# A Trainium2 encoder layer: three heads' attention in single buffers beside the projections instead of two, one head beside the Fourier branch instead of two

## The chip, the cores and the metric

The kernel runs on one core of a Trainium2 chip. The metric is the device time of one execution in microseconds (us). The kernel before takes 2184.91 us, the median of 3 runs (2184.82 to 2186.43). In the text PE is TensorE, DVE VectorE, ACT ScalarE, POOL GpSimd; SP is the engine that issues nearly all DMA transfers. Each engine works through its own instructions in order.

## What is computed

One layer of an encoder with 1024 tokens and width 1024, all in float32: a feed-forward block, a mixer, a second feed-forward block and a norm. The mixer has two branches, a Fourier transform over tokens and channels, and differential attention with four heads: each head has two components of width 64 with a softmax each, the second is subtracted from the first with a factor, and the difference weighs values of width 128.

```python
def diff_attention(q, k, v, positions, rel_bias, lam):
    ...
        s1 = jnp.einsum('bhqd,bhkd->bhqk', qblk[0], k[0]) * scale + bias
        s2 = jnp.einsum('bhqd,bhkd->bhqk', qblk[1], k[1]) * scale + bias
        attn = jax.nn.softmax(s1, axis=-1) - lam * jax.nn.softmax(s2, axis=-1)
        return jnp.einsum('bhqk,bhkv->bhqv', attn, vh)

def hybrid_mixer(h, ...):
    proj = h @ w_in
    u_f, q, k, v, g_a, g_b = jnp.split(proj, cuts, axis=-1)
    y_a = fourier_branch(u_f) @ w_fourier_out
    o = diff_attention(q, k, v, positions, rel_bias, lam)
    o = rms_norm(o, subln_g, SUBLN_EPS) * (1.0 - lambda_init)
    y_b = o.reshape(B, S, V_WIDTH) @ w_attn_out
    merged = jax.nn.sigmoid(g_a) * y_a + jax.nn.sigmoid(g_b) * y_b
    return merged @ w_out
```

## The kernel before

**Products.** Operands are split into a high part of 12 bits and the rest (`split`: a copy on ACT, L134, and a subtraction, L135, mostly on DVE), and a product takes three matmuls. The large products go by a form of Strassen's with seven block products (`seven_products`; its matmuls are L378, twelve to a product and half of the tokens, and DVE adds the results up in L386). `project(tiles, fn, cols, hook)` computes two tiles of 128 columns of `h @ w_in` for all tokens; after each of its seven products it calls `hook` once, which takes a step of a generator. So the generators' instructions are written between those of the products.

**What sets the order.** The written order is where a scheduler starts: it places each instruction on its engine by a timeline of its own, with waits where memory is reused. The order that results is fixed when the kernel is built. Memory has names: `xtile(j)` is x_j, `ntile(j)` n_j, `htile(j)` h_j; two things with one name can't live at once. `rh` hands out small tiles in turn.

**One tile of queries** (128 of the 1024, number g = 8 h + i of head h) takes these steps. `scores(g, c)`: matmuls of the component's queries and keys (L1148), on DVE the sum with the bias and its maximum (L1151), on ACT the exponentials (L1154). `combine(g)`: the factor (L1159, L1160), then s1 + factor s2, by ACT (L1165) and POOL (L1166), or for odd tiles of the later heads by DVE alone (L1163). `turn(g)`: eight transposes on PE (L1182) and a split. Then the weights by values: `weigh0`, one tile, 16 matmuls of 256 columns (L1224), summed (L1227, L1228) and stored to `o_d` in DRAM; or `weigh`, two tiles, 24 matmuls (L1195), and `back`, two transposes (L1206).

**Heads 0 and 1** run in `first_heads`, stepped by the hooks of the projections (8, 9), (2, 6), (3, 7), eight pairs of gates and (10, 11). Their exponentials stand in x5 and x6 for even tiles, x5 and x7 for odd ones, so that x5 has one tile at a time. **Head 2's** operands are made by `head_prep(2)` beside (12, 13), and its first tiles by `prime` beside (14, 15). `head_prep(h)` loads each half of queries and keys twice from DRAM (`twice`, L1075), copies it on ACT (L1083, L1092), subtracts on POOL (L1084, L1093), and transposes the values (L1113). It writes x0 to x4, for head 3 n4, n5 and x5.

**Heads 2 and 3** have four buffers (n0, n1, n2, n6) in turn and work beside the generator `fourier`, whose 40 steps `fill` spreads over their 16 tiles. The steps of `hgen` between them are `head_prep(3)` in head 2 and `early_norms` (the norms of heads 0 to 2) in head 3. Then come y_b, the gates and the merge (first matmul L562), the output projection and the second feed-forward block.

## Time and profile before

| | |
|---|---|
| median of 3 runs | 2184.91 us |
| the profiled execution, its span | 2188.2 us |
| PE busy | 2020.4 us, 92% |
| DVE busy | 1632.8 us, 75% |
| POOL busy | 1113.3 us, 51% |
| ACT busy | 951.0 us, 43% |

A profile records one execution with every instruction's start and end on each engine. Busy shares are means over the whole span, in which stages with different limits follow each other; the views by window and the timelines of the engines tell what holds in one stage. The seven products' L378 alone takes 1151.9 us of PE in 5256 matmuls. The granted clock is the mean of PE's clock, 1.00 being full.

### The profile page before, as it was taken

How to read it: one execution, taken by the hardware profiler on the slowest of the kernel's cores; microseconds unless marked ns; L12 is line 12 of the kernel's file. 1: busy time of each engine (PE TensorE's matmuls, PEld its weight loads, DVE VectorE, ACT ScalarE, POOL GpSimd, SP SyncE). 2: the span in 40 equal slices, each digit the busy share in tenths (PEclk: the TensorE clock that was granted, in tenths of full speed). 3: DMA queues.
4: the chain of work that ended last, by engine and by line, in shares of the span. 5: the costliest groups of instructions: out<-in, count | busy, mean ns of one | idle time of the engine just before them, and what ended most of it. 6: DMA issues, size and time to landing. Idle time of an engine off the chain costs nothing. (4 is left out here: it accounts for less than half of the span.)

```text
span 2188.2 us, 27538 instructions
## 1 busy us (share of the span) xinstructions
PE 2020.4 (92%) x9433; PEld 1642.4 (75%) x9433; DVE 1632.8 (75%) x2266; ACT 951.0 (43%) x1687; POOL 1113.3 (51%) x788
## 2 busy tenths in 40 slices
PE   5999999997988899999999799888999999979987
PEld 4987788875866777777776577667888888857775
DVE  8866566579897966666758987978766656598995
ACT  6423333233434544767646652345332333333345
POOL 5622233347579663343364652787432323275586
PEclk9999999999999899999999989999999999999998
DMA  4222511160421244353366547312222221151302
GB/s 139 89 85 85 149 52 55 57 221 0 132 71 53 87 150 130 98 168 94 111 190 205 160 133 273 107 66 82 75 82 82 72 58 58 56 185 49 121 15 87
DMA packets 155190, 228.90 MB, mean 105 GB/s; under 512 B 15968, under 2 KB 65280, under 8 KB 155048
## 3 DMA queue, kind: packets, MB, share of 16 engines
q1 hardware_dynamic: 148920, 215.85, 30.9%
q10 hardware_dynamic: 4608, 8.39, 1.0%
q0 software_dynamic: 1520, 2.88, 0.5%
q8 instruction: 75, 1.23, 0.2%
q14 instruction: 67, 0.55, 0.1%
HBM read 181.95 MB, written 49.31 MB: 106 GB/s over the span
## 5 line engine op out<-in xcount | busy, mean ns | idle before, releaser
L378 PE MATMUL p<-n,op 128*128 128x512 f32 (+1 forms) x5256 | 1151.9, 379 | 23.3 <-DVE r L386 11.3
L378 PEld LDWEIGHTS p<-n,op 128*128 128x128 f32 x5256 | 945.9, 191 | 214.6 <-issue 13.0
L134 ACT ACTIVATE op<-r 128x512 fp32r<-128x512 f32 x472 | 291.7, 628 | 556.6 <-PE p L378 255.6
L135 DVE TENSOR_TENSOR op<-r,op 128x512 fp32r<-128x512 f32 x453 | 398.7, 892 | 134.8 <-ACT op L134 129.7
L386 DVE TENSOR_TENSOR r<-p,r 128x512 f32<-128x512 f32 (+1 forms) x462 | 288.9, 639 | 270.9 <-PE p L378 265.8
L218 POOL TENSOR_TENSOR r<-r,r 128x512 f32<-128x512 f32 x189 | 276.8, 1474 | 246.9 <-DVE op L135 196.5
L562 PE MATMUL b<-n,op 128*128 128x512 f32 x1080 | 265.6, 402 | 41.3 <-DVE n L135 21.9
L562 PE MATMUL p<-n,op 128*128 128x512 f32 x1068 | 261.6, 403 | 28.5 <-DVE n L135 23.1
L562 PEld LDWEIGHTS b<-n,op 128*128 128x128 f32 x1080 | 204.4, 192 | 98.1 <-DVE n L135 33.0
L562 PEld LDWEIGHTS p<-n,op 128*128 128x128 f32 x1068 | 206.0, 195 | 79.0 <-DVE n L135 27.2
L222 POOL TENSOR_TENSOR r<-r,r 128x512 f32<-128x512 f32 x63 | 84.9, 1348 | 325.4 <-DVE x L774 80.2
L135 DVE TENSOR_TENSOR n<-n,n 128x512 fp32r<-128x512 f32 x142 | 174.7, 1239 | 4.7 <-ACT n L134 4.7
L503 POOL TENSOR_TENSOR n<-n,n 128x512 f32<-128x512 f32 x50 | 82.1, 1658 | 69.1 <-DVE n L135 28.7
L134 ACT ACTIVATE n<-n 128x512 fp32r<-128x512 f32 x156 | 95.3, 616 | 10.1 <-DVE n L1735 6.3
L1166 POOL TENSOR_TENSOR x<-x,x 128x1024 f32<-128x1024 f32 x16 | 38.8, 2426 | 109.8 <-ACT x L1165 101.7
L765 ACT ACTIVATE r<-r 128x512 f32<-128x512 f32 (+1 forms) x96 | 57.0, 596 | 84.8 <-DVE r L386 83.1
L134 ACT ACTIVATE op<-n 128x512 fp32r<-128x512 f32 x64 | 40.2, 629 | 99.5 <-PE b L562 41.7
L134 ACT ACTIVATE op<-x 128x512 fp32r<-128x512 f32 x68 | 42.8, 629 | 86.9 <-PE b L562 44.2
L591 POOL TENSOR_TENSOR n<-n,n 128x512 f32<-128x512 f32 x32 | 53.8, 1704 | 49.0 <-DVE n L597 49.0
L1148 PE MATMUL A<-x,x 128*128 128x512 f32 (+1 forms) x192 | 66.4, 432 | 6.5 <-ACT x L1092 4.1
L400 ACT ACTIVATE r<-p 128x512 f32<-128x512 f32 (+1 forms) x66 | 36.6, 555 | 71.7 <-PE p L378 68.7
L135 DVE TENSOR_TENSOR op<-x,op 128x512 fp32r<-128x512 f32 x58 | 57.8, 997 | 6.6 <-ACT op L134 6.5
(291 smaller groups left out, 2486.5 us busy)
## 6 DMA issues: line engine op xcount, KB each, us to landing
r<-in_ffn_wg SPq DMA_DIRECT2D x96, 256.0 KB
r<-in_ffn_wu SPq DMA_DIRECT2D x94, 256.0 KB
n<-in_ffn_wd SPq DMA_DIRECT2D x88, 256.0 KB
proj_d<-r SPq DMA_DIRECT2D x56, 256.0 KB
h_d<-r SPq DMA_DIRECT2D x32, 256.0 KB
rh<-proj_d SPq DMA_DIRECT2D x64, 128.0 KB
x<-bias_d SPq DMA_DIRECT2D x16, 512.0 KB
r<-in_w_gate SPq DMA_DIRECT2D x32, 256.0 KB
```

The lines of the kernel that those rows point to most:

```text
L134: act.activation(hi, src, AF.Copy)
L135: eng.tensor_tensor(out=lo, in0=src, in1=hi, op=ALU.subtract)
L218: pool.tensor_tensor(out=b[o], in0=b[x], in1=b[y], op=ALU.subtract)
L222: pool.tensor_tensor(out=b["s1"], in0=b[2], in1=b[3], op=ALU.add)
L378: pe.matmul(ps, lhsT=w[wi][:, d * P:(d + 1) * P], rhs=xn[b][xi][:, d, cols], start=(m == 0), stop=(m == 11))
L386: dve.tensor_tensor(out=o, in0=x, in1=y, op=ALU.add)
L503: eng.tensor_tensor(out=y, in0=v, in1=w, op=op)
L562: pe.matmul(ps[p], lhsT=wa[ai][:, p * P:(p + 1) * P], rhs=wb[bi], start=(j == 0 and m == 0), stop=(j == nj - 1 and m == 2))
L591: pool.tensor_tensor(out=new[1], in0=old[1], in1=v, op=ALU.add)
L765: act.activation(c, c, AF.Silu)
L1148: pe.matmul(ps[:, ns], lhsT=qq, rhs=kk[:, ns], start=(n == 0), stop=(n == 1))
L1166: pool.tensor_tensor(out=s1, in0=s2, in1=s1, op=ALU.add)
```

## The change

Three heads instead of two run in `first_heads`, in x5, x6, x7, with their sums stored to `o_d`; only head 3 has the four buffers and runs beside the Fourier branch, so `fill` spreads its 40 steps over 8 tiles. `head_prep(3)` stands at the end of `first_heads` and uses x0 to x4 like the other heads. A new hook `beside` takes 129 steps (as many as `first_heads` has) over the 91 hooks of 13 projections. The values (10, 11) are projected earlier, (12, 13) is among the 13; `prime` is now for head 3. `early_norms` runs from the start of the loop and loads three heads from `o_d`, into n7, n4, n5. The norms' results for heads 0 and 1 are in memory of their own (e0, e1, e2, and x5), no longer in x0 to x3. The weight stream is ordered like the products; a scratch memory for descriptors is set to 4096 bytes. All comments and docstrings are gone, which shifts line numbers by two or three. The diff without them:

```diff
+HEAD_STEPS = 129
+NB_HEADS = H - 1
...
-    o_d = dram.tile([2, TT, P, P], F32, name="o_d")
+    o_d = dram.tile([NB_HEADS, TT, P, P], F32, name="o_d")
...
-    for hp in (0, 4, 2, 3):
+    for hp in (0, 4, 2, 5, 3):
         qkv(hp, EARLY[2][3] if hp == 0 else "")
     for dm in range(DT):
         seven(lambda b, dm=dm: fetch(a["w_gate"][dm, b]))
-    qkv(5)
...
     def head_prep(h):
-        if h == 3:
-            two = [ntile(4 + j, [P, 2, S]) for j in range(2)]
-            stk[h] = [two[j // 2][:, j % 2, :] for j in range(4)] + [xtile(5, [P, S], F32R)]
-        else:
-            stk[h] = [xtile(j, [P, S], F32R) for j in range(5)]
+        stk[h] = [xtile(j, [P, S], F32R) for j in range(5)]
...
-    G0 = 2 * TT
+    G0 = NB_HEADS * TT
...
     def head_norm(h, halves=(0, 1)):
         if oT[h] is None:
-            oT[h] = [htile(q, [P, S]) if h == 2 else xtile(2 * h + q, [P, S], F32R) for q in range(2)]
+            oT[h] = [htile(q, [P, S]) if h == 2 else xtile(2 * h + q, [P, S], F32R) if h == 3 else
+                     T(big, f"e{2 * h + q}", [P, S], F32R) if h + q < 2 else xtile(5, [P, S], F32R) for q in range(2)]
...
     def early_norms():
-        o_first()
+        for k in range(H - 1):
+            o_s[k] = (o23[:, 0], *n45)[k]
+            sp.dma_start(out=o_s[k], in_=o_d[k].rearrange("t p c -> p t c"))
+        yield
         head_scale(0, (H - 1) * TT)
...
     def first_heads():
-        for _ in range(3):
+        for _ in range(6):
             yield
-        for h in range(2):
+        for h in range(NB_HEADS):
             yield from head_prep(h)
...
             weigh0(g0 + TT - 1)
             yield
+        yield from head_prep(NB_HEADS)
+
+    hgen = first_heads()
+    pace = [0, 0]
+
+    def beside():
+        pace[0] += 1
+        while pace[1] < pace[0] * HEAD_STEPS // (13 * NBLK):
+            pace[1] += 1
+            step(hgen)
...
-    hgen = first_heads()
-    project((8, 9), None, hook=each(hgen))
-    for h in range(2, H):
-        project((h, 4 + h), None, hook=each(hgen))
+    project((8, 9), None, hook=beside)
+    project((2, 6), None, hook=beside)
+    project((10, 11), None, hook=beside)
+    project((3, 7), None, hook=beside)
     for dm in range(DT):
-        project((16 + dm, 24 + dm), AF.Sigmoid, hook=each(hgen))
-    project((10, 11), None, hook=each(hgen))
-    for _ in hgen:
-        pass
-    hgen = head_prep(2)
-    project((12, 13), None, hook=each(hgen))
+        project((16 + dm, 24 + dm), AF.Sigmoid, hook=beside)
+    project((12, 13), None, hook=beside)
     for _ in hgen:
         pass
...
     project((14, 15), None, hook=each(prime()))
     o23 = ntile(7, [P, 2, TT, P], F32)
-    o_s[2], o_s[3] = o23[:, 0], o23[:, 1]
-
-    def o_first():
-        o01 = ntile(11, [P, 2, TT, P], F32)
-        for h in range(2):
-            sp.dma_start(out=o01[:, h], in_=o_d[h].rearrange("t p c -> p t c"))
-            o_s[h] = o01[:, h]
+    o_s[3] = o23[:, 1]
+    n45 = [ntile(j, [P, TT, P], F32) for j in (4, 5)]
...
     fgen = fourier()
-    hgen = head_prep(3)
+    hgen = early_norms()
...
     for g in range(G0 + 2, NG + 2):
         h, i = divmod(g, TT)
-        if i == 0 and g < NG:
-            if hgen is not None:
-                for _ in hgen:
-                    pass
-            hgen = head_prep(h + 1) if h + 1 < H else early_norms()
...
-        if g < NG and (i > 0 if h + 1 < H else i > 1):
+        if g < NG and i > 1:
             step(hgen)
...
-    nc = bacc.Bacc("TRN2", target_bir_lowering=False, num_devices=1)
+    nc = bacc.Bacc("TRN2", target_bir_lowering=False, num_devices=1, dynamic_dma_scratch_size=4096)
```

What that does to the order on the engines is shown at three places. A row is an instruction: its line, its operation, out<-in and the shape; the numbers behind a tile's name tell its uses apart.

The first is DVE around the last sum of the projections, the row of L386 that reads p_11050; the rows of L1151 are sums of scores, A being the scores. Before:

```order
L386 TENSOR_TENSOR r_1485_10927<-p_11050,r_1485_10927 128x512
L1151 ISA n_1512_11079,nms<-A_11167,n_1512_11079 128x1024
L1151 ISA nms 128x1
L1151 ISA n_1480_10904,nms<-A_11290,n_1480_10904 128x1024
L1151 ISA nms 128x1
L135 TENSOR_TENSOR n_1509_11064<-b_11065,n_1508_11063 128x4x128
L135 TENSOR_TENSOR n_1509_11064<-b_11072,n_1508_11063 128x4x128
L1151 ISA n_1480_10904,nms<-A_11297,n_1480_10904 128x1024
L1151 ISA nms 128x1
L1159 RECIPROCAL ccs<-l2s 128x1
L1151 ISA n_1481_10906,nms<-A_11368,n_1481_10906 128x1024
L1151 ISA nms 128x1
```

The same place after, where lines are moved (L388 is the sum of the projections, L1148 that of scores, L1156, L1157 the factor, L1225 and L1211 the end of `weigh0`):

```order
L1148 ISA x_1000_8102,nms<-A_10491,x_1001_8103 128x1024
L1148 ISA nms 128x1
L137 TENSOR_TENSOR h_1402_10476<-b_10477,h_1401_10475 128x512
L137 TENSOR_TENSOR h_1402_10476<-b_10484,h_1401_10475 128x512
L1148 ISA x_1001_8103,nms<-A_10547,x_1001_8103 128x1024
L1148 ISA nms 128x1
L388 TENSOR_TENSOR r_1576_11456<-p_11579,r_1576_11456 128x512
L1156 RECIPROCAL ccs<-l2s 128x1
L1157 SCALAR_TENSOR_TENSOR ccs<-l1s,ccs,nlam 128x1
L1225 TENSOR_TENSOR rh_10515<-b_10498,rh_10515 128x128
L1211 ISA junk_10518,oss<-rh_10515 128x128
L1211 ISA oss 128x1
```

Before, sums of scores of three buffers (n_1512, n_1480, n_1481) follow each other there, between them the split of a transposed tile. After, one tile's two sums are in x_1000 and x_1001 (x5 and x6), and the end of `weigh0` of a tile of head 2 follows.

The second is POOL where head 3's operands are made: L1084 and L1093 subtract for queries and keys, L1166 combines a tile, L1283 to L1301 are the Fourier branch's folds. Before:

```order
L1166 TENSOR_TENSOR n_1480_10904<-n_1480_10904 128x1024
L1283 MEMSET r_1566_11337 128x512
L1283 MEMSET r_1567_11338 128x512
L1084 TENSOR_TENSOR n_1523_11123<-rh_11231,n_1523_11123 64x512
L1084 TENSOR_TENSOR n_1523_11123<-rh_11236,n_1523_11123 64x512
L1093 TENSOR_TENSOR x_1525_11125<-rh_11309,n_1524_11124 64x512
L1295 COPY r_1573_11395<-r_1566_11337 128x1
L1093 TENSOR_TENSOR x_1525_11125<-rh_11314,n_1524_11124 64x512
L1296 TENSOR_TENSOR r_1573_11395<-r_1566_11337,r_1567_11338 128x511
L1300 TENSOR_TENSOR r_1574_11398<-r_1573_11395,r_1567_11338 128x1 x2
L1301 TENSOR_TENSOR r_1574_11398<-r_1573_11395 128x255 x2
L1166 TENSOR_TENSOR n_1489_10947<-n_1489_10947 128x1024
```

After, with the same subtractions in L1085 and L1094, combines in L1163:

```order
L1163 TENSOR_TENSOR x_1000_8102<-x_1001_8103,x_1000_8102 128x1024
L1163 TENSOR_TENSOR x_1000_8102<-x_1002_8104,x_1000_8102 128x1024
L1085 TENSOR_TENSOR x_1537_11281<-rh_11286,x_1537_11281 64x512
L1085 TENSOR_TENSOR x_1538_11282<-rh_11291,x_1538_11282 64x512
L1085 TENSOR_TENSOR x_1537_11281<-rh_11322,x_1537_11281 64x512
L1085 TENSOR_TENSOR x_1538_11282<-rh_11327,x_1538_11282 64x512
L1094 TENSOR_TENSOR x_1541_11285<-rh_11332,x_1539_11283 64x512
L1094 TENSOR_TENSOR x_1541_11285<-rh_11337,x_1540_11284 64x512
L1094 TENSOR_TENSOR x_1541_11285<-rh_11362,x_1539_11283 64x512
L1094 TENSOR_TENSOR x_1541_11285<-rh_11367,x_1540_11284 64x512
L1163 TENSOR_TENSOR n_1571_11433<-n_1571_11433 128x1024
L1163 TENSOR_TENSOR n_1580_11476<-n_1580_11476 128x1024
```

Before, the subtractions stand one or two at a time among the folds and the combines of head 2. After, all eight stand in a row, behind the combines of head 2's last two tiles, which are in x5 (x_1000), and ahead of the first combine of head 3.

The third is SP at the same preparation, after; L1076 is `twice`, its two loads in one row, L1227 stores a tile of `weigh0`, L1107 loads values:

```order
L1227 DMA o_d<-rh_11023 128x128
L1227 DMA o_d<-rh_11120 128x128
L149 DMA r_1725_12273<-proj_d 128x512
L149 DMA r_1726_12275<-proj_d 128x512
L1076 DMA rh_11286<-proj_d 64x512 x2
L1227 DMA o_d<-rh_11257 128x128
L1076 DMA rh_11291<-proj_d 64x512 x2
L1076 DMA rh_11322<-proj_d 64x512 x2
L1531 DMA n_1606_11614<-o_d 128x8x128
L1076 DMA rh_11327<-proj_d 64x512 x2
L1076 DMA rh_11332<-proj_d 64x512 x2
L1076 DMA rh_11337<-proj_d 64x512 x2
```

The first pair of loads stands ahead of the store of head 2's last tile (rh_11257), the other seven behind it. Before, the pairs for head 3 stand among the loads of the bias, with no such store near them.

## Rows read from the trace of the kernel before

**Rows 1.** The page: span; TensorE's busy time, share, instructions, and its weight loads.

```profile
span 2188.2 us, 27538 instructions
...
PE 2020.4 (92%) x9433; PEld 1642.4 (75%) x9433; DVE 1632.8 (75%) x2266; ACT 951.0 (43%) x1687; POOL 1113.3 (51%) x788
```

**Rows 2.** Busy us (instructions) by engine and window, granted clock, DMA share, GB/s.

```profile
794.55:1169.40 374.85, 369.01 (x1728) 289.38 (x1729) 251.66 (x399) 218.77 (x340) 162.14 (x123) 1.00 0.46 143
1169.40:1259.70 90.30, 72.81 (x378) 53.24 (x377) 82.08 (x146) 57.80 (x113) 56.09 (x62) 0.90 0.53 164
1259.70:1384.60 124.90, 115.15 (x563) 92.47 (x564) 100.62 (x179) 46.55 (x84) 58.66 (x44) 0.92 0.56 193
1169.40:1384.60 215.20, 187.95 (x940) 145.72 (x939) 182.70 (x324) 104.36 (x197) 114.75 (x106) 0.91 0.55 181
```

**Rows 3.** PE's timeline: start us, us, what; both ends of the second stretch.

```profile
1166.35 3.03 PE L378 MATMUL p<-n,op 128*128 128x512 f32 x12
1169.22 1.04 PE L1182 MATMUL b<-ident,n 128*128 128x128 f32 x8
...
1384.62 7.64 PE L562 MATMUL p<-n,op 128*128 128x512 f32 x33
```

**Rows 4.** PE's timeline of one tile of head 1 beside the projections.

```profile
1043.41 1.28 PE L1148 MATMUL A<-x,x 128*128 128x512 f32 x4
1044.62 1.09 PE L1182 MATMUL b<-ident,x 128*128 128x128 f32 x8
1045.47 5.72 PE L378 MATMUL p<-n,op 128*128 128x512 f32 x24
...
1052.22 2.17 PE L1224 MATMUL b<-h,h 128*128 128x256 f32 x16
1054.23 5.63 PE L378 MATMUL p<-n,op 128*128 128x512 f32 x24
```

**Rows 5.** DVE, ACT and POOL, same tile, and the next's first sum.

```profile
1045.84 1.22 DVE L1151 CUSTOM_DVE_ANT_0 x<-A,x 128x1024 f32<-128x1024 f32 x1 [0.82 <-PE b L1182]
...
1061.23 1.22 DVE L1151 CUSTOM_DVE_ANT_0 x<-A,x 128x1024 f32<-128x1024 f32 x1
...
1047.71 1.16 ACT L1154 ACTIVATE x<-x,nms 128x1024 f32<-128x1024 f32 x1
...
1049.45 1.15 ACT L1154 ACTIVATE x<-x,nms 128x1024 f32<-128x1024 f32 x1
...
1051.24 1.15 ACT L1165 ACTIVATE x<-x,ccs 128x1024 f32<-128x1024 f32 x1 [0.55 <-DVE ccs L1160]
...
1052.47 2.40 POOL L1166 TENSOR_TENSOR x<-x,x 128x1024 f32<-128x1024 f32 x1 [4.28 <-ACT x L1165]
```

**Rows 6.** PE, ACT, POOL and DVE where head 0 gives way to 1.

```profile
956.52 2.08 PE L1224 MATMUL b<-h,h 128*128 128x256 f32 x16
958.44 13.79 PE L378 MATMUL p<-n,op 128*128 128x512 f32 x60
...
960.21 0.63 ACT L1083 ACTIVATE x<-rh 128x512 fp32r<-128x512 f32 x1 [1.29 <-DMA rh<-proj_d]
...
976.57 0.63 ACT L1092 ACTIVATE x<-rh 128x512 fp32r<-128x512 f32 x1 [2.94 <-DMA rh<-proj_d]
...
979.13 1.60 POOL L1093 TENSOR_TENSOR x<-rh,x 64x512 fp32r<-64x512 f32 x1
...
982.91 1.21 DVE L1151 CUSTOM_DVE_ANT_0 x<-A,x 128x1024 f32<-128x1024 f32 x1
```

**Rows 7.** Timelines of DVE and POOL around a combine on POOL.

```profile
1185.36 0.15 DVE L1383 TENSOR_TENSOR col<-col,r 128x1 f32<-128x1 f32 x1
...
1189.95 2.32 DVE L1383 TENSOR_TENSOR col<-col,r 128x1 f32<-128x1 f32 x1
...
1189.22 3.03 POOL L1166 TENSOR_TENSOR n<-n 128x1024 f32<-128x1024 f32 x1 [6.90 <-ACT n L1165]
```

**Rows 8.** By window, 20 us of the second stretch.

```profile
1180.00:1200.00 20.00, 15.52 (x81) 13.40 (x81) 16.87 (x36) 10.38 (x21) 10.28 (x12) 0.76 0.46 134
```

## The prediction

> **What bounds the kernel now.** I read the page first. TensorE (PE) is busy 92% of the span [rows 1], but an average over stages doesn't say what an edit in one stage is worth. So I cut the mixer's attention into stretches with the view of busy times by window [rows 2], at points taken from PE's timeline [rows 3]. Beside the last projections (794.55 to 1169.40 us) PE is busy 369.01 of 374.85 us at a granted clock of 1.00: PE bounds this stretch, and what VectorE (DVE), ScalarE (ACT) and GpSimd (POOL) do there is hidden. Behind the last projection product (1169.40 to 1384.60) PE is busy only 187.95 of 215.20 us while DVE is busy 182.70. In the first 90.30 us of it, up to just ahead of the transposes of head 3's first tile, DVE is busy 82.08 us (91%) and PE 72.81: there DVE is nearest to the bound. In the next 124.90 us PE has 115.15 and DVE 100.62.
>
> The change means to move a head's attention from the second stretch, where PE waits, to the first, where PE never waits. So the question is whether the head gets there, and what is left behind the last projection.
>
> **Whether the third head gets beside the projections.** A tile of the first heads is a chain through all engines. DVE's sum of scores and bias for the first component starts at 1045.84, ACT takes the exponentials from 1047.71 to 1050.6, scales from 1051.24, POOL adds from 1052.47 to 1054.87 [rows 5]: 9.03 us. Then PE has to transpose, and only then may the next tile's scores be written, since all these tiles share x5. In PE's queue two projection products of 12 + 12 matmuls stand in the gap twice per tile (5.72 and 5.63 us [rows 4]), so a tile takes 15.4 us here: 1045.84 to 1061.23 [rows 5]. That pace fills the projections already. The order that was built says the same: from the first scores to the last projection product PE has 1128 projection matmuls (94 products) in both kernels, beside them 19.5 tiles' scores before and 19 after. There is no extra room: about four products pass per tile, before and after. The table of steps asks for three heads, but five tiles of head 2 come behind the last projection, still in the shared buffers, as the fences of the change show. **What the change moves is thus not work out of the PE-poor stretch but the kind of tile in it**: before, two-buffered pairs of tiles of heads 2 and 3, throughout; after, first single-buffered ones, a preparation of head 3 in the open, then pairs.
>
> **Cost beside the projections.** Against before, this stretch has 16 more matmuls of weights by values (272 for 256), 16 more transposes (144 for 128), 4 fewer of scores (152 for 156). From start to start [rows 4]: 16 of the first take 2.01 us (1052.22 to 1054.23), 8 transposes 0.85 (1044.62 to 1045.47), 4 scores 1.21. Sum +2.0 + 1.7 − 1.2 = **+2.5 us**, all on the bound engine. The next stretch is as much lighter: its count of matmuls is 936 for 940.
>
> **Cost behind the last projection, up to head 3's first transposes** (before: 90.30 us, 378 matmuls; after: 376 matmuls by the order, so the same points can be compared):
> - Six tiles' ends come there (the tile in flight and five more). A period without projection products is the chain, 9.03, and the transposes, 1.1 (8 of them [rows 4]): 10.1. Below 9.4 it can't go if only half the transposes hold the next scores up; 12 if Fourier work stands in the queues as projection products do now. The first three have Fourier steps between them in the order, for which I add 1.5 each. 6 × 10.1 + 4.5 = 65.1; the tile in flight has about 2.7 behind it: **62.4**.
> - The last tile's transposes, split and weighing until its store: 0.85 + 2.01 [rows 4] and about a microsecond for the split, **4**.
> - Head 3's preparation. Before, it is spread over head 2 and hidden. After, it wants x0 to x4, which head 2 holds to its last scores; POOL does its eight subtractions in a row behind the last two combines, and on SP only one of the eight pairs of loads stands ahead of the store of head 2's last tile. The nearest rows are the switch from head 0 to head 1 [rows 6]: from the end of the last weighing (956.52 + 2.08 = 958.60) to DVE's first sum of the new head, 982.91, are 24.3 us, of which the eight copies and subtractions take 20.5 (960.21 to 979.13 + 1.60); ACT waits for the loads there (1.29 us before the first copy, 2.94 before the last). PE was covered by 60 projection matmuls meanwhile; that cover is gone. From below: one load and copy (1.61 + 0.63) and eight subtractions of 1.60 make 15. I take **20**, as there is less between the steps than in the rows.
> - The first tile's chain to its transposes: 9.0 and up to one microsecond, **10**.
>
> Together 62.4 + 4 + 20 + 10 = 96.4 against 90.3: **+6**. Bounds: 6 × 9.4 − 2.7 + 4 + 15 + 9 = 82 (no Fourier step in the way), and 6 × 12 + 1.8 + 4 + 24.3 + 11 = 113.
>
> **The rest, to the merge's first matmul** (1384.62 [rows 3]): 560 matmuls after, 563 before, which took 124.9 us. The Fourier branch's 40 steps are now spread over 8 tiles. DVE, freed in the serial part, has more left: counting the order's rows by the mean times of their lines I estimate 109 us against 100.62. That still is below PE's, but the two wait for each other more. I take 127, **+2**; between 120, if it gets nearer to PE's busy time, and 135, if DVE's 109 keep the share that it has now (100.62 of 124.9).
>
> **What costs nothing.** The norms of heads 0 to 2 start earlier and read three heads from DRAM: one more load on SP and 8 stores that the projections and tiles cover. The weight stream of the keys moves with its products. From the output projection on, PE has the same order; the rearranged x tiles let loads start earlier, and no row shows PE there waiting for one. [...]
>
> Sum: +2.5 + 6 + 2 = **+10.6** on the profiled 2188.2, which stands 3.3 above the median of 2184.91. On the median's scale: 2195.5.
>
> [...] DVE's combine of odd tiles is gone from the tiles that are now single-buffered: about four more combines behind the last projection are POOL's, of 2.4 us each. The trace shows what DVE meets then: a subtraction with both inputs in SBUF takes 2.32 us at 1189.95 under POOL's combine (1189.22 to 1192.25), and 0.15 us at 1185.36 without one [rows 7]. [...]
>
> **Rivals.**
> - Faster. What stands against the forecast is that DVE is busy for 91% of the first stretch now. If the chains run at their own pace, with Fourier steps really in the gaps, the first stretch takes 86 (near the lower bound), the rest goes at 120 because fewer pairs of tiles press on DVE: −4.3 − 4.9 + 2.5 = −6.7, 2178. It decides for faster when the time behind the last projection falls below 208 us. Against it: the serial chain and the eight-step preparation alone fill over 80 us.
> - The same. Tiles trade places at equal price, 90 and 125, and only the 2.5 us of matmuls remain: 2187.5.
> - Much slower. The open preparation takes its full 24 us, the periods go to 12 because POOL's combines block DVE (2.32 us for 0.15 [rows 7]), and PE, with gaps, runs at a lower granted clock: it shows 0.76 between 1180 and 1200 already [rows 8]. 110 and 133: +19.7 + 8.1 + 2.5 = +30, 2215.
> - The third head does get beside the projections, as the table of steps asks. Then 8 tiles leave a stretch of 12.5; but the order has only 19 tiles there, so I give it nothing of its own; it is in the chance for faster.
>
> **How the numbers follow.** A measurement of this kernel can tell about 0.2% from no change, 4.4 us: same is 2180.5 to 2189.3. Chances: forecast (2189.3 to 2206) 0.45, much slower (2206 to 2222) 0.14, same 0.18, faster 0.23. So slower 0.59. Leaving out the far half of much slower and the far half of faster (together 0.18), the range is 2176 to 2213. It holds cases of both signs; the likeliest alone spans 2189.3 to 2206.
>
> **What would show it.** The sums of scores behind the last projection write x6 and x7 with 10 to 12 us between tiles; eight subtractions of the preparation stand in a row on POOL, with ACT waiting for the loads and PE idle, its granted clock low; DVE's share of the first stretch falls under 91% and rises in the second; 20 to 25 us pass between head 2's last weighing and head 3's first sum. I am wrong if PE stays busy through that switch, if a period is much below 10 us, or if the rest takes less than 120 us; and if the time differs outside 794.55 to 1384.62 by more than a few microseconds, a step is missing.

## The result: 2246.3 us, slower by 2.8%

The changed kernel takes 2246.3 us, the median of 4 runs (2241.52 to 2250.34), the kernel before 2184.86 us beside it. The ratio is 1.0277, with a 95% interval of 1.0253 to 1.0301. The forecast said slower and put 2195.5 us and at most 2213 on it; the loss is 61 us where 10.6 were summed up.

The page of the changed kernel, its span and TensorE's line (busy us, share, instructions), beside [rows 1]:

```profile
span 2247.4 us, 27616 instructions
...
PE 2061.7 (92%) x9457; PEld 1671.0 (74%) x9457; DVE 1624.2 (72%) x2270; ACT 953.0 (42%) x1689; POOL 1119.4 (50%) x792
```

TensorE's share is 92% again, and it is busy 41 us longer, for 24 more matmuls: part of the matmuls ran slower. Where, is told by the windows (columns as in [rows 2]): from the first scores to the end of the last projection product, from there to head 2's last transposes, to head 3's first, to the merge, and the last three together:

```profile
806.70:1176.10 369.40, 364.59 (x1721) 286.65 (x1722) 246.43 (x393) 213.12 (x334) 161.30 (x121) 0.99 0.44 136
1176.10:1259.21 83.11, 56.24 (x258) 43.72 (x256) 54.46 (x106) 37.76 (x70) 45.78 (x55) 0.72 0.42 134
1259.21:1303.97 44.76, 36.85 (x116) 21.84 (x116) 18.69 (x41) 23.66 (x43) 12.46 (x9) 0.61 0.31 89
1303.97:1449.93 145.96, 129.92 (x566) 102.59 (x565) 97.68 (x177) 47.21 (x85) 59.09 (x45) 0.83 0.55 184
1176.10:1449.93 273.83, 223.00 (x938) 168.15 (x936) 170.83 (x324) 108.63 (x197) 117.33 (x109) 0.76 0.47 153
```

- Beside the projections: 369.40 us. Cut in the same way, from the first scores at 805.70 to 1169.40 us, the kernel before takes 363.70 (its line stands below). +5.7 us, 2.5 were forecast.
- From the last projection to head 3's first transposes: 83.11 + 44.76 = 127.9 us for 90.30 [rows 2], +37.6, 6 were forecast.
- From there to the merge: 145.96 for 124.90, +21.1, 2 were forecast.

Together +64.4. Before the first scores lies 1.0 more, and behind the merge 6.1 less (797.5 for 803.6 us), which makes the 59.2 between the spans of 2247.4 and 2188.2. Those 6.1 are scatter: the kernel of experiment 4, with the same order there, takes 803.9 from the merge on. The kernel before, beside its projections:

```profile
805.70:1169.40 363.70, 360.75 (x1694) 283.10 (x1695) 244.96 (x392) 215.14 (x333) 157.28 (x120) 1.00 0.45 140
```

Behind the last projection TensorE is busy 223.00 us for 187.95 before and idle 50.8 for 27.3, at a granted clock of 0.76 for 0.91: of the 58.6 us that this stretch is longer, 35 show as slower matmuls and 23.6 as gaps. DVE, the engine that was nearest to the bound, is less busy than before: 170.83 of 273.83 us. So the chain is what got longer, not an engine's work.

The periods of the single-buffered tiles are read from TensorE's timeline (start us, us, what), in the starts of L1179, the transposes:

```profile
1173.19 3.01 PE L380 MATMUL p<-n,op 128*128 128x512 f32 x12
...
1189.04 1.91 PE L1179 MATMUL b<-ident,x 128*128 128x128 f32 x8
...
1205.62 1.91 PE L1179 MATMUL b<-ident,x 128*128 128x128 f32 x8
...
1222.98 1.83 PE L1179 MATMUL b<-ident,x 128*128 128x128 f32 x8 [2.21 <-POOL x L1163]
...
1237.67 1.97 PE L1179 MATMUL b<-ident,x 128*128 128x128 f32 x8 [2.52 <-POOL x L1163]
...
1248.47 1.10 PE L1179 MATMUL b<-ident,x 128*128 128x128 f32 x8 [2.17 <-POOL x L1163]
...
1259.21 1.97 PE L1179 MATMUL b<-ident,x 128*128 128x128 f32 x8 [3.82 <-POOL x L1163]
```

From 1189.04 to 1237.67 a tile takes 16.6, 17.4 and 14.7 us; there Fourier steps stand between the tiles, in the third of these periods only on the other engines. The last two, with none, take 10.8 and 10.7, as worked out from the chain (10.1).

Then the switch, in rows of TensorE, DVE, POOL and ACT:

```profile
1264.50 2.07 PE L1221 MATMUL b<-h,h 128*128 128x256 f32 x16
...
1277.86 0.77 PE L1145 MATMUL A<-x,x 128*128 128x512 f32 x1 [3.28 <-POOL x L1085]
...
1287.89 16.15 PE L1145 MATMUL A<-x,x 128*128 128x512 f32 x28
1303.97 1.97 PE L1179 MATMUL b<-ident,n 128*128 128x128 f32 x8
...
1285.50 1.23 DVE L1148 CUSTOM_DVE_ANT_0 n<-A,n 128x1024 f32<-128x1024 f32 x1 [12.05 <-PE A L1145]
...
1271.19 3.97 POOL L1085 TENSOR_TENSOR x<-rh,x 64x512 fp32r<-64x512 f32 x3 [12.04 <-ACT x L1084]
1276.61 1.26 POOL L1085 TENSOR_TENSOR x<-rh,x 64x512 fp32r<-64x512 f32 x1 [1.45 <-ACT x L1084]
1277.84 2.60 POOL L1094 TENSOR_TENSOR x<-rh,x 64x512 fp32r<-64x512 f32 x2
1282.05 1.26 POOL L1094 TENSOR_TENSOR x<-rh,x 64x512 fp32r<-64x512 f32 x1 [1.61 <-ACT x L1093]
1283.93 1.27 POOL L1094 TENSOR_TENSOR x<-rh,x 64x512 fp32r<-64x512 f32 x1 [0.63 <-ACT x L1093]
1296.27 2.36 POOL L1163 TENSOR_TENSOR n<-n 128x1024 f32<-128x1024 f32 x1 [11.07 <-ACT n L1162]
...
1275.90 0.63 ACT L1084 ACTIVATE x<-rh 128x512 fp32r<-128x512 f32 x1 [2.12 <-DMA rh<-proj_d]
...
1281.34 0.63 ACT L1093 ACTIVATE x<-rh 128x512 fp32r<-128x512 f32 x1 [2.25 <-DMA rh<-proj_d]
```

Head 2's last weighing starts at 1264.50. POOL's eight subtractions (3 + 1 + 2 + 1 + 1) go from 1271.19 to 1285.20, and ACT waits for the loads of `rh` before copies, 2.12 and 2.25 us here: the open preparation, as forecast. What the forecast did not have is the row at 1287.89: head 3's first transposes (1303.97) stand behind 28 matmuls of scores, of all four buffers, and these take 16.15 us, 0.58 each. Beside the projections four of them took 1.21 us from start to start [rows 4], 0.30 each. The window there shows the clock:

```profile
1280.00:1300.00 20.00, 17.61 (x37) 8.40 (x36) 9.64 (x19) 12.00 (x18) 5.33 (x4) 0.50 0.17 48
```

The granted clock is 0.50, for 1.00 beside the projections [rows 2], after waits such as the 3.28 us before 1277.86; at this clock TensorE is busy 17.61 of 20 us with only 37 matmuls.

And the Fourier branch stands still there. L1495 is its last kind of product, by the output weights; six matmuls of it, then none until the last row here. L1439 is the step before, the transform over the channels:

```profile
1263.11 1.56 PE L1439 MATMUL p<-x,r 128*128 128x512 f32 x4
...
1272.91 1.67 PE L1495 MATMUL p<-n,n 128*128 128x512 f32 x6
...
1341.58 0.95 PE L1439 MATMUL b<-n,r 128*128 128x512 f32 x3
1342.36 0.39 PE L1439 MATMUL b<-x,r 128*128 128x512 f32 x1
...
1349.35 1.15 PE L1495 MATMUL p<-x,n 128*128 128x512 f32 x4
```

That is 75 us. What the product waits for are the four matmuls at 1341.58: its other operands are made from their results. They stand in TensorE's order behind head 3's first tiles, 77 us behind the two sums that the kernel writes just ahead of them (ended at 1264.67). In the kernel before they (L1441) stand with the rest of the branch, and the same product, L1497, goes on at once:

```profile
1250.10 0.86 PE L1441 MATMUL b<-n,r 128*128 128x512 f32 x3
...
1261.35 2.91 PE L1497 MATMUL p<-n,n 128*128 128x512 f32 x6
1264.06 1.76 PE L1497 MATMUL p<-x,n 128*128 128x512 f32 x4
```

### The profile page after: what moved, and what is told of

The parts are those of the page before. It is cut to its first block, busy times and chain, and to the rows that moved or that the text cites. A ratio compares the mean times of both kernels' runs of the same rounds, so it can differ in the third digit from the quotient of the medians.

```text
span 2247.4 us, 27616 instructions
## 1 busy us (share of the span) xinstructions
PE 2061.7 (92%) x9457; PEld 1671.0 (74%) x9457; DVE 1624.2 (72%) x2270; ACT 953.0 (42%) x1689; POOL 1119.4 (50%) x792
## 5 line engine op out<-in xcount | busy, mean ns | idle before, releaser
L380 PE MATMUL p<-n,op 128*128 128x512 f32 (+1 forms) x5256 | 1152.4, 379 | 22.4 <-DVE r L388 10.6
L388 DVE TENSOR_TENSOR r<-p,r 128x512 f32<-128x512 f32 (+1 forms) x462 | 289.1, 639 | 262.5 <-PE p L380 258.6
L137 DVE TENSOR_TENSOR n<-n,n 128x512 fp32r<-128x512 f32 x142 | 180.4, 1279 | 4.9 <-ACT n L136 4.9
L1163 POOL TENSOR_TENSOR x<-x,x 128x1024 f32<-128x1024 f32 x24 | 57.2, 2382 | 124.8 <-ACT x L1162 114.9
L1145 PE MATMUL A<-x,x 128*128 128x512 f32 (+1 forms) x256 | 102.8, 501 | 15.4 <-ACT x L1093 7.0
L136 ACT ACTIVATE n<-n 128x512 fp32r<-128x512 f32 x156 | 95.3, 616 | 10.1 <-DVE n L1733 6.3
L1145 PEld LDWEIGHTS A<-x,x 128*128 128x128 f32 (+1 forms) x256 | 47.8, 220 | 55.6 <-issue 38.6
L593 POOL TENSOR_TENSOR n<-n,n 128x512 f32<-128x512 f32 x32 | 53.8, 1705 | 49.2 <-DVE n L599 49.2
```

The source lines that it names most:

```text
L136: act.activation(hi, src, AF.Copy)
L137: eng.tensor_tensor(out=lo, in0=src, in1=hi, op=ALU.subtract)
L380: pe.matmul(ps, lhsT=w[wi][:, d * P:(d + 1) * P], rhs=xn[b][xi][:, d, cols], start=(m == 0), stop=(m == 11))
L388: dve.tensor_tensor(out=o, in0=x, in1=y, op=ALU.add)
L593: pool.tensor_tensor(out=new[1], in0=old[1], in1=v, op=ALU.add)
L1145: pe.matmul(ps[:, ns], lhsT=qq, rhs=kk[:, ns], start=(n == 0), stop=(n == 1))
```

## The experiments

Eleven kernels. Each was run in turn with the kernel before on the same chip, one of them (7) only once; where a stretch is given, it is from the profiled run. The fences show the part of an edit that the text speaks of; `...` at an end marks that more places are changed, mostly memory that makes room.

**1. Two buffers** (e1_two_buffers). The shared x5 is taken away.

```diff
-                t = [xtile(5 + j, [P, S]) for j in range(3)]
-                sc[0], sc[1] = t[:2], t[::2]
+                t = [xtile(5 + j, [P, S]) for j in range(3)] + [T(big, "e0", [P, S])]
+                sc[0], sc[1] = t[:2], t[2:]
```

> The changed kernel, but odd tiles of the first three heads have their exponentials in x7 and e0 instead of x5 and x7, so that two tiles can be on their way at once (e0 is free until the norms). In the order all 24 tiles' scores of three heads then stand beside the projections, instead of 19. Theory 1, the shared buffer is what leaves five tiles of head 2 and head 3's preparation in the open: the stretch beside the projections grows by its added matmuls (40 scores, 32 transposes, 73 weights by values: about 25 us), the six serial periods (83 us) and most of the open preparation (45 us) go, some 40 to 50 us of Fourier work that stood among them stay; 2170 to 2205 us. Theory 2, the third head costs its time wherever it stands: within 10 us of the changed kernel's 2246.

Measured: 2206.5 us (2204.47 to 2215.02), 40 less than the changed kernel, just above what theory 1 gave (2205); against the kernel before 1.0116 (1.0077 to 1.0155). The two stretches, beside the projections and behind them:

```profile
802.30:1193.00 390.70, 390.70 (x1867) 304.43 (x1868) 273.69 (x448) 237.74 (x373) 172.92 (x126) 0.99 0.45 140
1193.00:1400.80 207.80, 175.59 (x792) 135.31 (x791) 143.21 (x269) 83.13 (x158) 107.04 (x104) 0.81 0.55 182
```

All 24 tiles are beside the projections now. That costs 21.3 us against the changed kernel's 369.40, where 25 were estimated, and 27.0 against the 363.70 of the kernel before, with TensorE busy in all of 390.70. The stretch behind falls to 207.80, below the 215.20 of the kernel before by 7.4 only, though 4.5 tiles have gone from it. So the shared buffer is what leaves five tiles in the open, and yet mending it doesn't pay.

**2. Head 3's operands in other memory** (e2_prep_hidden).

```diff
-        stk[h] = [xtile(j, [P, S], F32R) for j in range(5)]
+        if h == 3:
+            two = [ntile(4 + j, [P, 2, S]) for j in range(2)]
+            stk[h] = [two[j // 2][:, j % 2, :] for j in range(4)] + [T(big, "e2", [P, S], F32R)]
+        else:
+            stk[h] = [xtile(j, [P, S], F32R) for j in range(5)]
...
```

> The changed kernel, but head 3's operands are written to n4, n5 and e2 and not to x0 to x4 (sums of heads 1 and 2 then in x0 and x1, norms' results in e0, e1, x4, x5): one part of the change undone, so that the preparation needs not wait for head 2's last scores. If the open preparation is a loss of its own, the 37 us between head 2's last weighing and head 3's first transposes shrink to 10 or 15 us: 2212 to 2226 us. If it is hidden by something else or only exchanged for another wait, 2235 to 2250.

Measured: 2244.3 us (2239.13 to 2248.91), no gain. But it doesn't decide the question: in its order the eight subtractions still stand behind head 2's last combine, since they are written behind it. Other memory alone doesn't bring them forward. Experiment 8 does.

**3. The last stage's memory alone, in the kernel before** (e3_before_memory).

```diff
-            oT[h] = [htile(q, [P, S]) if h == 2 else xtile(2 * h + q, [P, S], F32R) for q in range(2)]
+            oT[h] = [htile(q, [P, S]) if h == 2 else xtile(2 * h + q, [P, S], F32R) if h == 3 else
+                     T(big, f"e{2 * h + q}", [P, S], F32R) if h + q < 2 else xtile(4, [P, S], F32R) for q in range(2)]
...
-    nc = bacc.Bacc("TRN2", target_bir_lowering=False, num_devices=1)
+    nc = bacc.Bacc("TRN2", target_bir_lowering=False, num_devices=1, dynamic_dma_scratch_size=4096)
```

> The kernel before with the last part of the change alone: the norms' results of heads 0 and 1 in e0, e1, e2 and x4 instead of x0 to x3, and the small scratch memory for descriptors that makes room for them. The changed kernel gains back about 8 us in the output projection against its own lag; if the freed x tiles (earlier loads there) are why, this takes 2176 to 2180 us; if it is something of the third head, 2185 as before.

Measured: 2180.81 us, median of 10, against 2183.87, median of 13; ratio 0.9992 (0.9976 to 1.0009). No difference that can be told: the rearranged memory and the smaller scratch are worth between a gain of 5 us and a loss of 2. The stretch behind the last projection, 213.40 for 215.20, is the same kernel's again:

```profile
1167.20:1380.60 213.40, 192.00 (x941) 147.47 (x939) 180.87 (x328) 104.51 (x197) 115.44 (x106) 0.89 0.55 185
```

**4. The gaps filled** (e4_fill). 128 matmuls whose results nobody reads, behind head 2's last weighings (`warm`; 16 per tile, 48 behind the last).

```diff
+    def warm(g, n):
+        hi, lo = dts[g]
+        v = vs[2][0]
+        ps = bank()
+        for k in range(n):
+            pe.matmul(ps, lhsT=v[:, 0, 0:P], rhs=hi[:, 0:4, :].rearrange("p a c -> p (a c)"), start=True, stop=True)
...
```

> The changed kernel with 128 idle matmuls (128x512, results never read) behind the weighings of head 2's last tiles, where TensorE waits; nothing else moves in the order. Theory: the low granted clock (0.66 in the serial stretch, 0.50 at head 3's first scores) is a loss of its own, as scores, transposes and weighings are links of the serial chain: with the gaps filled the granted clock rises above 0.85 there and 15 to 25 us go, 2221 to 2231 us. Rival: the waits of the chain set the time and the clock only fills idle time: 2246 or, as the idle matmuls take up to 29 us, up to 2260.

Measured: 2244.85 us (2238.21 to 2246.99), the changed kernel's time. The windows, cut as the first three of the changed kernel behind its projections:

```profile
1173.60:1252.37 78.77, 63.09 (x337) 49.47 (x335) 49.92 (x107) 37.48 (x72) 46.48 (x55) 0.91 0.44 145
1252.37:1292.98 40.61, 36.94 (x164) 25.97 (x164) 22.40 (x39) 23.73 (x43) 12.61 (x9) 0.96 0.30 87
1292.98:1439.30 146.32, 129.72 (x565) 102.90 (x565) 97.88 (x180) 47.45 (x85) 59.21 (x45) 0.81 0.54 186
```

The granted clock rose as expected, from 0.72 to 0.91 and from 0.61 to 0.96 in the first two stretches. They got shorter by 4.3 and 4.2 us (78.77 for 83.11, 40.61 for 44.76), and the total shows no difference. So the low clock goes with the waits, and filling these gives back some 8 us, not the theory's 15 to 25. That much is net: the idle matmuls stand in the same queue and take time too (sixteen of them 3.82 us, at 1193.73), and behind 1292.98, where none were put, the clock stays low (0.81) and the time the same. What the clock alone costs is thus not shown; that most of the 35 us of slower matmuls was time in which TensorE would have waited otherwise is the likelier reading.

**5. The Fourier branch's memory** (e5_fourier_memory). Its first results share x6 and x7 with the scores of the first heads, now until head 2's end.

```diff
-        A = [xtile(6, [P, 2, 512], F32R), xtile(7, [P, 2, 512], F32R), n12[:, 0], n12[:, 1], n13[:, 0]]
+        A = [T(big, "e0", [P, 2, 512], F32R), T(big, "e1", [P, 2, 512], F32R), n12[:, 0], n12[:, 1], n13[:, 0]]
...
```

> The changed kernel with two places swapped: the Fourier branch's first results (its operands X and E0) in e0 and e1 instead of x6 and x7, which head 2's tiles hold until their end; the norms' results of head 0 in x6 and x7, of head 3 in e0 and e1. Theory: the Fourier branch stands still behind its token transforms (no step of it on TensorE from 1219 to 1260 us) because its results may not be written while head 2 uses x6 and x7; freed, it works on beside the serial tiles and 15 to 30 us go: 2215 to 2231 us. Rival: the branch is tied to head 3's tiles by the pace of its steps anyway: 2238 to 2250.

Measured: 2251.89 us (2245.81 to 2257.67), no gain; from the last projection to the merge:

```profile
1171.30:1443.75 272.45, 215.30 (x936) 162.29 (x935) 173.04 (x324) 108.74 (x197) 117.61 (x109) 0.79 0.46 154
```

272.45 for 273.83. The branch's next steps do come earlier, but then it stops at the same product, and for longer: the four matmuls of L1439 stand at 1334.61 here, behind head 3's first tiles as before. The rival's time was right.

**6. Both of these** (e6_both). Experiment 1 with the branch's results in e1 and e2.

```diff
-        A = [xtile(6, [P, 2, 512], F32R), xtile(7, [P, 2, 512], F32R), n12[:, 0], n12[:, 1], n13[:, 0]]
+        A = [T(big, "e1", [P, 2, 512], F32R), T(big, "e2", [P, 2, 512], F32R), n12[:, 0], n12[:, 1], n13[:, 0]]
...
```

> Two buffers as in e1_two_buffers, and the Fourier branch's first results out of the score buffers (e1, e2). With all 24 tiles beside the projections, only the last tiles' ends stand in the branch's way, some 10 us: 2196 to 2206 us. If the branch's memory is the larger cause and shared buffers the smaller, under 2190.

Measured: 2208.49 us (2203.33 to 2212.76), as in experiment 1. This memory is no cause by itself.

**7. The Fourier branch without a head beside it** (e7_fourier_alone). In experiment 1's kernel the loop over head 3's tiles keeps only the steps of the branch and of the norms.

```diff
-        if g - 1 < NG:
-            combine(g - 1)
-        if g < NG:
-            scores(g, 0)
-            scores(g, 1)
         fill(g, 0)
...
+    pool.memset(o_s[3], 1.0)
...
```

> e1_two_buffers with head 3 left out: its preparation, scores, combines, transposes and weighings are not computed, its sums are set to one; the Fourier branch, the norms, y_b and all that follows stay. It measures what the Fourier branch takes with no head beside it. In e1_two_buffers the time from the last projection to the merge is 207.8 us. Theory: the branch's own chain of steps and the tail of y_b hold it up, so that without head 3 it is still 175 us or more. Rival: TensorE's and VectorE's work sets it; then the missing head's matmuls (about 45 us) and its wait for the preparation take it to 140 us or less.

Measured: 2149.02 us, in one run. Beside the projections and behind them:

```profile
806.30:1196.90 390.60, 389.96 (x1866) 303.56 (x1867) 272.80 (x447) 237.67 (x373) 172.88 (x127) 1.00 0.45 141
1196.90:1352.00 155.10, 123.88 (x553) 99.12 (x551) 101.68 (x178) 40.58 (x84) 88.90 (x92) 0.87 0.59 196
```

155.10 us: between the two theories. From it come prices. Head 3 beside the branch adds 207.80 − 155.10 = 52.7 us in experiment 1, and the heads' work in the kernel before adds 215.20 − 155.10 = 60.1. Beside the projections, experiment 1 added 27.0 us to the kernel before. Divided by the tiles whose scores stand there, 12.5 and 4.5, these would be 4.8 and 6.0 us a tile. But the two numbers are not of the same tiles: beside the projections experiment 1 has, by the trace, 36 matmuls of scores more (4.5 tiles), but also 46 transposes (5.75 tiles) and 91 matmuls of weights by values (5.7 tiles). At the times of [rows 4] these are 10.9 + 4.9 + 11.4 = 27.2 us, all of the 27.0. Set against TensorE's added busy time, the two places cost alike: 27.0 us for 29.9 (390.70 − 360.75), 60.1 for 64.1 (187.95 − 123.88). No run shows that the branch's waits hide a part of a tile.

**8. The preparation inside head 2** (e8_prep_inside). Experiment 2, with the steps written between head 2's last tiles.

```diff
                 turn(g)
+                if 2 * TT + 3 <= g <= 2 * TT + 6:
+                    if g == 2 * TT + 3:
+                        prep = head_prep(NB_HEADS)
+                    next(prep)
                 yield
             weigh0(g0 + TT - 1)
             yield
-        yield from head_prep(NB_HEADS)
+        yield from prep
...
```

> The changed kernel with head 3's preparation in n4, n5 and e2 (as in e2_prep_hidden), and now also written between head 2's last tiles, one step per tile, as the kernel before does; in the order its subtractions then stand among head 2's combines, and head 3's scores right behind head 2's last ones. Theory: the open preparation costs 25 to 30 us of its own (44.8 us from head 2's last transposes to head 3's first, about 15 here): 2214 to 2224 us. Rival: head 2's tiles get slower by as much, or the time is lost again behind: 2235 to 2250.

Measured: 2223.11 us (2215.06 to 2233.47), 23 less than the changed kernel; 1.0202 (1.0159 to 1.0246) of the kernel before. The stretch behind the last projection, and the transposes of head 2's last tile and head 3's first:

```profile
1169.50:1409.30 239.80, 199.76 (x937) 153.09 (x936) 170.93 (x324) 107.37 (x197) 118.90 (x109) 0.85 0.52 173
...
1257.10 1.10 PE L1183 MATMUL b<-ident,x 128*128 128x128 f32 x8
...
1274.53 1.03 PE L1183 MATMUL b<-ident,n 128*128 128x128 f32 x8
```

239.80 for 273.83, and 17.4 us from one head's transposes to the other's for 44.8. The open preparation is a loss of its own: 27 us between the transposes and 34 in the stretch of the profiled run, which is the fastest of the four; 23 by the medians.

**9. Fourier steps ahead** (e9_fourier_first). Experiment 5, and

```diff
+    for _ in range(18):
+        filled[0] += 1
+        step(fgen)
     for g in range(G0 + 2, NG + 2):
...
-        while filled[0] < (2 * (g - G0) + k - 2) * FOURIER_STEPS // (2 * (NG - G0)):
+        while filled[0] < 18 + (2 * (g - G0) + k - 2) * (FOURIER_STEPS - 18) // (2 * (NG - G0)):
```

> e5_fourier_memory, and 18 of the Fourier branch's 40 steps written ahead of head 3's loop, the other 22 spread beside its tiles. Theory: what is left of the branch is pressed into head 3's eight tiles, so that the time from head 3's first transposes to the merge is 143 to 146 us for 125 in the kernel before; with the steps ahead it is 125 to 130, 2228 to 2236 us. Rival: the steps wait for the same memory and engines, 2245 to 2258.

Measured: 2233.68 us (2227.73 to 2240.2), as the theory had it, 18 less than experiment 5.

```profile
1176.80:1427.76 250.96, 203.54 (x937) 153.97 (x937) 172.44 (x324) 107.98 (x197) 118.28 (x109) 0.83 0.51 167
```

250.96 for 272.45: the branch pressed into head 3's eight tiles costs some 21 us of the stretch. From head 3's first transposes (1305.92) to the merge are 121.8 us now, for 146.0 in the changed kernel. The branch still stops behind the first six matmuls of that product; the four matmuls that it waits for stand at 1309.74. What moving them alone would give was not tried.

**10. All three** (e10_all_three). Experiment 8 with the branch's results in e0 and e1 and 18 of its steps ahead, as in 5 and 9; the norms' results then are in these places:

```diff
+            names = ("x6", "x7"), ("x4", "x5"), ("h0", "h1"), ("e0", "e1")
+            oT[h] = [T(big, names[h][q], [P, S], F32R) for q in range(2)]
...
```

> The changed kernel with all three at once: the preparation inside head 2's last tiles (e8_prep_inside), the Fourier branch's first results in e0 and e1 (e5_fourier_memory), and 18 of its steps ahead. If the three causes add up, the 34 us of e8_prep_inside and some 15 us more go behind the last projection: 2200 to 2212 us. If the unbuffered tiles beside which the steps now stand get slower by as much, 2218 to 2230.

Measured: 2203.01 us (2200.35 to 2205.44), 43 less than the changed kernel; 1.0089 (1.0069 to 1.0109) of the kernel before.

```profile
1174.80:1405.21 230.41, 201.59 (x936) 157.39 (x936) 176.50 (x326) 106.34 (x197) 120.05 (x109) 0.84 0.55 180
```

230.41 for 273.83. The causes add up for the most part: 43 us in the stretch of 34 + 21, and 43 by the medians of 23 (experiment 8) + 18 (experiment 9 against 5).

**11. All of it with two buffers** (e12_two_buffers_all). Experiment 6, with 18 steps ahead and the preparation written behind head 2's last scores:

```diff
                 scores(g, 1)
+                if g == G0 - 1:
+                    prep = head_prep(NB_HEADS)
+                    next(prep)
+                    next(prep)
                 yield
                 combine(g)
+                if g == G0 - 1:
+                    next(prep)
+                    next(prep)
...
```

> The other two causes mended where the shared buffer is mended as well: e6_both, with 18 of the Fourier branch's steps ahead and head 3's preparation written right behind head 2's last scores. If moving a whole head beside the projections is worth it once nothing stands in the open, this beats the kernel before: 2165 to 2180 us. If a tile costs as much beside the projections (27 us for 4.5 tiles in e1_two_buffers against the kernel before, 6 each) as it takes beside the Fourier branch (60 us for 12.5 tiles, from e7_fourier_alone's 155 us to the 215 of the kernel before, 4.8 each), it can at best come near it: 2183 to 2198 us.

Measured: 2192.17 us (2189.68 to 2195.33) against 2180.96; 1.0052 (1.0034 to 1.007). The fastest of the kernels with three heads beside the projections, and still 0.5% slower than the kernel before:

```profile
803.00:1192.00 389.00, 388.14 (x1867) 302.06 (x1866) 270.99 (x448) 237.08 (x373) 171.78 (x125) 1.00 0.45 140
1192.00:1384.92 192.92, 166.83 (x791) 128.60 (x791) 146.68 (x269) 83.64 (x158) 108.22 (x104) 0.86 0.60 196
```

Against the kernel before, the stretch beside the projections is 389.00 − 363.70 = 25.3 us longer and the stretch behind them 215.20 − 192.92 = 22.3 shorter: what the move takes away in one place it adds in the other, together 581.9 us for 578.9. The four matmuls of L1439 stand from 1253.56 on here, among the branch's other sums, and its product goes on without a stop. By the medians the whole is 11 us longer, by the profiled runs (2187.9 and 2188.2) not at all, so differences of a few us between such stretches decide nothing. No kernel here that computes all four heads beats the one before by more than its measurement is uncertain.

## Why the prediction was right in sign and wrong in size

The measured stretches stand 53.8 us above the sum of 10.6. By the prediction's terms these are 20.7 in the six periods (83.1 for 62.4), 10.8 in the switch between the heads (44.8 for 34), 19 in the rest (146 for 127) and 3.2 beside the projections (5.7 for 2.5).

**Right.** The bound beside the projections and that the third head doesn't fit there: 19 of 24 tiles, five more behind the last projection, in x5 to x7. That the change doesn't move work out of the stretch but makes it serial there. A bare period of 10.1 us (10.7 and 10.8). The open preparation as a separate loss, its eight subtractions in a row, ACT's waits for the loads (2.12 and 2.25 us), the low clock (0.72 and 0.61): each was seen, and experiment 8 shows what the open preparation costs. That the memory of the last stage is worth nothing that can be measured (experiment 3). That 19 tiles fit was right by the order, not by the pace: at 15.4 us a tile the 363.7 us would hold 23.6.

**The periods with Fourier steps.** The term "1.5 each" for the steps between the tiles was mis-sized: 16.6, 17.4 and 14.7 us for 10.1 are 4.6 to 7.3 each. The stretch of six tiles took 83.1 for 62.4 us. The 1.5 came from no row. In a serial chain a step in the queue of any of four engines lies in the way, and the chain's own matmuls ran slower there (eight transposes 1.91 us for 1.09 in [rows 4], at a granted clock of 0.72 in this stretch for 1.00).

**The switch.** "4 + 20 + 10" from head 2's last transposes to head 3's first were 44.8. They are 7.4 to the end of the weighing (1266.57), 18.9 to the first sum (1285.50) and 18.5 to the transposes. The preparation itself came out near the term (the weighing starts at 1264.50, the last subtraction ends at 1285.20). The step that failed is the last, "the first tile's chain to its transposes, 10": POOL's addition for this tile ends at 1298.63, 13.1 us behind the first sum where 9.0 were taken, and the transposes wait 5.3 us more in TensorE's queue. I compared the two kernels at the same count of matmuls, 376 for 378, and did not look at which they were. 36 of them are scores of head 3 that stand ahead of its first transposes, and the last 28 ran at a granted clock of 0.50 in 16 us. The order told the first; the second had its row in [rows 8], at 0.76.

**The rest.** "127, +2" was 146. This step failed by its method: I reasoned from busy time, 560 matmuls for 563 and DVE's 109 us, as if the work could be laid out anew. DVE was busy 97.68 us, not 109, 67% of the stretch and not more than before, against what I said would be seen. What sets the time is where the Fourier branch's steps stand: with its 40 steps tied to eight tiles, it stood still for 75 us and was then pressed into what was left. Experiment 9 moves 18 steps and takes 21 us away. The distance was in the order: six matmuls of the product, the next of them some 190 matmuls on, and shortly ahead of these the four on which they depend. Why the order has those four so late is open; in experiments 7 and 11 and in the kernel before they are not.

**The projections.** "+2.5" was +5.7: the three counts were right, but the profile also has more gaps, such as

```profile
1151.73 4.47 PE L380 MATMUL p<-n,op 128*128 128x512 f32 x12 [2.28 <-DVE r L388]
```

2.28 us for a sum on DVE. The windows have TensorE idle for 4.8 of 369.40 us, for 3.0 before; the rest of the difference I can't place.

**The rivals.** "Much slower" (2215, 14%) had the right mechanism, the open preparation at its full price, long periods, and the low clock, and too small a price; its own bounds ended at 2222. What it gave to POOL's combines is seen: a subtraction on DVE under a combine on POOL (the row of [rows 7] at 1189.95 is an addition),

```profile
1200.17 2.42 DVE L137 TENSOR_TENSOR n<-r,n 128x512 fp32r<-128x512 f32 x1 [0.81 <-ACT n L136]
...
1202.59 0.68 DVE L137 TENSOR_TENSOR op<-p,op 128x512 fp32r<-128x512 f32 x1
...
1218.93 0.68 DVE L137 TENSOR_TENSOR op<-r,op 128x512 fp32r<-128x512 f32 x1
...
1203.32 2.50 PE L1398 MATMUL p<-n,op 128*128 128x256 f32 x10 [2.05 <-DVE op L137]
...
1199.70 2.35 POOL L1163 TENSOR_TENSOR x<-x,x 128x1024 f32<-128x1024 f32 x1 [4.74 <-ACT x L1162]
```

takes 2.42 us and ends 0.54 us behind the combine; one of the same shape, at 1218.93 with nothing running on POOL, takes 0.68 us. In [rows 7] the addition took 2.32 us for 0.15. The longer subtraction is not free here: behind it on DVE stands the subtraction for which TensorE waits 2.05 us, and behind TensorE's matmuls of 1203.32 stand the tile's transposes (1205.62), though its combine ended at 1202.05. That DVE was idle for 28.7 of the 83.11 us does not show the opposite, as the chain waits for it at such places. How much of the 20.7 us in excess comes from this no run shows. For the clock's part, filling the gaps gave back 8 us (experiment 4). "Faster" fell with its condition, that the chains run at their own pace.

**What was not asked.** Whether a tile is cheaper in one place than in the other at all. The runs show no difference: in both the time added is nine tenths or a little more of TensorE's added busy time (27.0 of 29.9 us beside the projections, 60.1 of 64.1 behind them). So even with all in place (experiment 11) the moved head gains nothing. The price beside the projections could have been read ahead from [rows 4]: 1.21 for the scores of each component, 0.85 and 2.01 make 5.3 us a tile.

The 58.6 us behind the last projection are thus shown in parts: the open preparation (34.0 in experiment 8's profile, 23 by the medians), the branch tied to eight tiles (21.5, experiment 9 against 5; 18 by the medians), both together 43.4 (experiment 10); 15.2 remain over the kernel before. Experiment 11 speaks for the unbuffered tiles there: it has five tiles less in the stretch than experiment 10, 26.5 us at 5.3 each, but falls by 37.5 from its 230.41, so that some 11 are left for the buffers and for the branch's stop, which is gone too. No run parts them further.

## What to carry to other kernels

Price a piece of work in both places before it is moved, and count the same instructions in both: here the move took 22.3 us from one stretch and put 25.3 into the other (experiment 11, with all else mended), so that it did not pay. When an order is compared at two points, look at which instructions stand between them and how long each generator stands still, not at counts and busy shares: a serial stretch makes everything late that is tied to what comes after it, and four late matmuls held a whole branch for 75 us here. And a low granted clock beside gaps may be a sign of the gaps more than a cause; filling them brought the clock back here (0.72 to 0.91 and 0.61 to 0.96, experiment 4) and hardly any time (8.5 of 127.9 us).

## What was not expected of the hardware

That the clock could be brought back at so little gain: 128 matmuls more raised the granted clock from 0.72 to 0.91 and from 0.61 to 0.96, and the two stretches together got shorter by 8.5 us, though sixteen of the scores that had taken 0.58 us each at 0.50 now took 5.49 us, 0.34 each. And how much the part behind the merge scatters between runs: 797.5 us in the changed kernel's profile and 803.9 in experiment 4's, for the same order, as much as some effects that I had looked for there.
